# Short-convolution mixer by Strassen products: product 5 of the out-projection in seven parts, with new orders and earlier splits

## The chip, the cores and the metric

The kernel runs on one NeuronCore of a Trainium2 chip. The metric is the time of one execution on the device in microseconds (us), here the median of three runs.

## The reference

What is computed, with T = 1024 tokens and D = 2048 channels, all in float32:

```python
h = rmsnorm(x, norm0_w)
proj = h @ w_in                                   # 2048 x 8192
b_gate, c_gate, u, z = jnp.split(proj, 4, axis=-1)
cu = c_gate * u
conv = causal_depthwise_conv3(cu, w_conv)         # over tokens
y = b_gate * conv * jax.nn.silu(z)
x = x + y @ w_out                                 # 2048 x 2048
return rmsnorm(x, norm_f_w)
```

## The kernel before

All matrix products run on TensorE with float32 operands that are split in two (a rounded high part `h` and the rest `l`); each product is three passes, high x high, low x high, high x low (`PASSES`). `split` makes the parts: ScalarE casts the high part (L113), VectorE subtracts it from the source (L114). A split tile has the form `hl`: two times 1024 columns.

The program is a list of **steps**. A step is 24 matmuls of 128x128 weights on 512 columns, with hooks for its loads, its sums of weights (`add`), its splits, its matmuls and the evacuation of its PSUM banks. The main loop at the end of the kernel calls the loads of a step several steps ahead, its sums four and its splits three steps ahead, then the matmuls and the evacuation of the step itself. After each step it also runs two pieces of `background` work and, in phase 0, one `chore` that prepares later operands. A scheduler then fixes, when the program is built, the order of the instructions on each engine and which buffer each tile gets; each engine runs its own list in that order. Buffers of 4 KB per partition come from the pool `t4` (16), split tiles from `xp` (14, tokens) and `wp` (3, weights), PSUM tiles from 8 banks.

- **In-projection.** The first channel block (c = 0) runs in 8 steps by plain products (L370). Blocks c = 1 to 15 follow twice, in phase 0 for one half of the contraction and in phase 1 for the other, each as seven Strassen products in the order `PRODUCTS` = 1, 5, 6, 2, 7, 3, 4 (L483). The weight of product 5 is the difference `wt` = `wi_01 - wi_00`, made by VectorE (L117); that of product 6 is made from `wt`, that of product 4 in the same tile later. Phase 0 writes the four gate tiles `g` of a block to DRAM (`pd`), phase 1 loads them again and adds its own part from the banks `pa`, `pb`, `pc` (L120).
- **Gating.** When block c of phase 1 is done, `gating(c, g)` goes into `background` and is worked off in the next block: `g_0` times `g_1` (L218), three taps of the convolution (L221 on ScalarE, L225 twice on VectorE), L232, the sigmoid of `g_2` (L231 on ScalarE), L235 that multiplies `g_2` by it, and L238. The sigmoid lies in the tile `g_0`, so L235 is the last to read `g_0`. The result goes to `y_dram`; every second block adds sums of token columns and writes them to `s_dram`, every fourth (c = 3, 7, 11, 15) loads those of the other blocks and makes the sums `z` for the second level (256 columns each, L117 and L120), which go to `zd`.
- **Out-projection.** Products of the first level: 1, 6, 7 and 5, each for two column halves `db` as four steps `out_step` (L601). Products 2, 3 and 4 are taken a second level down, as seven products `out_second` (L670), a step each. So there are 32 + 21 = 53 steps. A step `out_step` loads a weight tile `wo` (512 KB) and a token tile `ys` (512 KB) and splits both; a step `out_second` loads `yz` (512 KB) and two `wz` (512 KB each) and splits all three. Results are added to the output rows `st` (L120), squared for the final norm (L557), and when the last column chunk of a row block has come, `finish` (L753 to L768) makes the scale and stores the rows.
- **Start.** The norm weights `n0` are loaded on ScalarE's queue (L81), tokens `xr` and first weights `wi_c` on SyncE's; ScalarE scales and casts the tokens (L349, needs `n0`), VectorE makes their low part (L350) and splits the weights (L355, L356).

Of the kernel before, what the change touches and what calls it, by code (L numbers as in the profile page):

```python
# [13 lines left out]
P = 128  # L14
# [29 lines left out]
def hybrid_kernel(  # L44
# [36 lines left out]
    nc.scalar.dma_start(n0, norm0_w)  # L81
# [6 lines left out]
    nc.scalar.activation(table, idle[:, 0:1], AF.Sigmoid)  # L88
# [124 lines left out]
    def gating(c, g):  # L213
# [32 lines left out]
        if c == 0:  # L246
            return parts
        if c % 2 == 0:
            kept[c] = gb
            return parts  # L250
# [4 lines left out]
        def s12():  # L255
            add(gc[:, u], e[:, v], gb[:, v])
            sub(gc[:, v], gc[:, u], e[:, u])
            nc.gpsimd.dma_start(sd[:, 0:2], gc.rearrange("p (i n) -> p i n", i=2))

        def s34():  # L260
            sub(gu[:, u], e[:, u], e[:, v])
            sub(gu[:, v], gb[:, u], gc[:, v])
            nc.gpsimd.dma_start(sd[:, 2:4], gu.rearrange("p (i n) -> p i n", i=2))

        if c % 4 == 1:
            return parts + [s12, s34]
        q = {}

        def before():
            q["y"], q["s"] = f4(f"zy_{c}"), f4(f"zs_{c}")  # L270
            nc.sync.dma_start(q["y"], y_dram[c - 2])
            nc.sync.dma_start(q["s"][:, 0:NB], s_dram[c // 4, 0][:, 3])

        def second(z):
            def f():
                t = {2: None, 3: gz, 4: gc}[z]
                if t is None:
                    t = f4(f"z_{c}")
                a = {2: q["y"][:, u], 3: q["s"][:, u], 4: q["y"][:, v]}[z]
                b = {2: gb[:, u], 3: gu[:, v], 4: gb[:, v]}[z]  # L280
# [9 lines left out]
        return [before] + parts + [s12, s34, second(3), second(2), second(4)]  # L290
# [6 lines left out]
    def classical():  # L297
# [241 lines left out]
    ycols = (slice(0, NB), slice(NB, T))  # L539
    yv = y_dram.rearrange("(u j h) p t -> h p u j t", j=2, h=2)  # L540
    sv = s_dram.rearrange("u j p s t -> u p j s t")

    to_come, pending = {}, {}
# [5 lines left out]
    def result(th, tb, chunk, ps):  # L549
# [7 lines left out]
        nc.scalar.activation(idle, v, AF.Square, accum_out=sums[th, tb][:, chunk:chunk + 1])  # L557
        weighs = pending.setdefault((th, tb), [])
        if len(weighs) == 3:
            for f in weighs:  # L560
                f()
            finish(th, tb, chunk)
            return
# [8 lines left out]
        scaled.append(weigh)  # L572

    def out_step(r, db, u):
# [3 lines left out]
        def loads():  # L578
            w["b"] = f4(f"wo_{db}_{r}_{u}")
            nc.sync.dma_start(w["b"], w_out[db, 0, 0, u] if r == 1 else t_dram[r][db, u])  # L580
            w["y"] = f4(f"ys_{db}_{r}_{u}")
            src = yv[0, :, u, :, ycols[0]] if r == 1 else sv[u, :, :, S_SLOT[r]]
            nc.sync.dma_start(w["y"].rearrange("p (j t) -> p j t", j=2), src)

        def split_w():
# [10 lines left out]
        def mm():  # L596
            open_banks()
            for jj in range(2):
                for tb in range(4):
                    for yz, wz in PASSES:  # L600
# [4 lines left out]
                            start=(r in (1, 5) and u == 0 and jj == 0 and yz == 0 and wz == 0),  # L605
                            stop=(r in (7, 5) and u == 3 and jj == 1 and yz == 1),
# [266 lines left out]
```

## Time and profile before

| | |
|---|---|
| median of 3 runs | 1541.2 us (1541.03 to 1541.26) |
| the profiled execution | 1541.5 us |
| its span, first to last instruction | 1539.7 us |
| TensorE busy | 1523.5 us, 99% of the span |
| VectorE busy | 1143.7 us, 74% |
| ScalarE busy | 542.0 us, 35% |
| DMA | 351.95 MB, 229 GB/s over the span |

The profiled execution is 1.8 us longer than its span, and 0.3 us above the median. Busy shares are means over the whole span; a wait of TensorE, in the list of waits, is time in which its next matmul was held up by the named instruction of another engine.

### The profile page before, as it was taken

To read this page: it belongs to the slowest core of one execution; us is meant where nothing else is said; L and a number is where in the kernel's file an instruction comes from. 1 tells how busy PE (TensorE), PEld (TensorE's weight loads), DVE (VectorE), ACT (ScalarE), POOL (GpSimd) and SP (SyncE) were. 2 spreads that over 40 slices of the span, in tenths; PEclk is the share of its full clock that TensorE was granted. 3 is DMA by queue.
4 is the path that set the end of the run, shared out by engine and by line. 5 is a ranking of instruction groups with operands and counts; after the bars stand their busy time and mean duration, and the time that the engine had idled before them with its cause. 6 is when DMAs were issued, how large, how long until landed. Compare 5 with 4: busy or idle time off the path is not lost.

```text
span 1539.7 us, 17753 instructions
## 1 busy us (share of the span) xinstructions
PE 1523.5 (99%) x6705; PEld 1257.5 (82%) x6705; DVE 1143.7 (74%) x1321; ACT 542.0 (35%) x660; POOL 128.2 (8%) x234
## 2 busy tenths in 40 slices
PE   9999999999999999999999999999999999999997
PEld 7878888888888888888888888888888887888885
DVE  6798776677666565457888878887888786687787
ACT  5454444333333333322222222222222334454574
POOL 0001111111111110110000000000000120000000
PEclk9999999999999999999999999999999999999998
DMA  9605677998866674894346434543454679877772
GB/s 362 254 25 205 229 265 266 390 372 331 336 240 251 218 254 157 313 398 150 126 142 203 151 117 139 202 155 112 163 179 164 242 253 385 302 239 233 237 275 109
DMA packets 114277, 351.95 MB, mean 229 GB/s; under 512 B 11008, under 2 KB 22288, under 8 KB 112400
## 3 DMA queue, kind: packets, MB, share of 16 engines
q1 hardware_dynamic: 81040, 223.38, 42.9%
q0 software_dynamic: 31712, 122.72, 20.6%
q10 hardware_dynamic: 1440, 4.73, 0.8%
q8 instruction: 52, 0.85, 0.2%
q14 instruction: 33, 0.27, 0.0%
HBM read 243.83 MB, written 106.96 MB: 228 GB/s over the span
## 4 chain that ended last, share of the span: by engine, by line
PE 90%; DMA 5%; DVE 4%; issue 1%; ACT 1%; SPq 0%; POOL 0%; POOLq 0%; DVEq 0%; ACTq 0%
PE pa L483 42%; PE pc L483 21%; PE pb L483 11%; PE po L601 9%; PE po L670 7%; DMA xsq<-in_x_dram 2%; DMA wz<-in_w_out_dram 1%; DMA xr<-in_x_t_dram 1%; DVE X L114 1%; DVE xr L148 0%; DVE st L120 0%; DVE xc L350 0%; DVE g L397 0%; DMA wi_c<-in_w_in_dram 0%; DVE st L569 0%
## 5 line engine op out<-in xcount | busy, mean ns | idle before, releaser
L483 PE MATMUL pa<-X,w 128*128 128x512 f32 x2880 | 667.8, 389 | 1.1 <-ACT w L113 1.1
L483 PEld LDWEIGHTS pa<-X,w 128*128 128x128 f32 x2880 | 540.5, 188 | 113.8 <-ACT w L113 1.6
L483 PE MATMUL pc<-X,w 128*128 128x512 f32 x1440 | 336.5, 389 | 0.7 <-ACT w L113 0.7
L483 PEld LDWEIGHTS pc<-X,w 128*128 128x128 f32 x1440 | 270.2, 188 | 57.2 <-ACT w L113 1.1
L114 DVE TENSOR_TENSOR w<-wi,w 128x1024 fp32r<-128x1024 f32 x150 | 183.2, 1222 | 146.5 <-ACT w L113 145.5
L113 ACT CAST w<-wi 128x1024 fp32r<-128x1024 f32 x150 | 157.0, 1050 | 229.3 <-PE pa L483 131.4
L601 PE MATMUL po<-wo,Y 128*128 128x512 f32 x768 | 177.5, 389 | 0.9 <-DVE wo L114 0.9
L601 PEld LDWEIGHTS po<-wo,Y 128*128 128x128 f32 x768 | 144.1, 188 | 31.2 <-DVE wo L114 1.4
L483 PE MATMUL pb<-X,w 128*128 128x512 f32 x720 | 168.1, 389 | 0.0
L483 PEld LDWEIGHTS pb<-X,w 128*128 128x128 f32 x720 | 135.1, 188 | 28.1
L113 ACT CAST w<-wt 128x1024 fp32r<-128x1024 f32 x60 | 63.3, 1055 | 234.5 <-PE pc L483 120.2
L120 DVE TENSOR_TENSOR g<-pa,g 128x512 f32<-128x512 f32 x150 | 102.4, 685 | 29.3 <-PE pa L483 28.1
L670 PE MATMUL po<-wzh,Yz 128*128 128x512 f32 x504 | 117.3, 389 | 0.0
L670 PEld LDWEIGHTS po<-wzh,Yz 128*128 128x128 f32 x504 | 94.6, 188 | 19.6
L509 ACT COPY g<-pa 128x512 f32<-128x512 f32 x90 | 52.8, 587 | 138.0 <-PE pa L483 137.7
L117 DVE TENSOR_TENSOR wt<-wi,wi 128x1024 f32<-128x1024 f32 x60 | 73.3, 1222 | 26.7 <-DMA s_dram<-g 14.6
L370 PE MATMUL pc<-xc,wc 128*128 128x512 f32 x384 | 87.9, 390 | 0.9 <-DVE wc L355 0.9
L370 PEld LDWEIGHTS pc<-xc,wc 128*128 128x128 f32 x384 | 71.8, 188 | 17.4 <-issue 1.8
L114 DVE TENSOR_TENSOR w<-wt,w 128x1024 fp32r<-128x1024 f32 x60 | 73.1, 1219 | 10.0 <-ACT w L113 10.0
L120 DVE TENSOR_TENSOR g<-pc,g 128x512 f32<-128x512 f32 x90 | 61.4, 684 | 23.4 <-PE pc L483 23.0
L114 DVE TENSOR_TENSOR wzh<-wz,wzh 128x1024 fp32r<-128x1024 f32 x42 | 50.9, 1219 | 21.2 <-ACT wzh L113 21.1
L120 DVE TENSOR_TENSOR st<-po,st 128x512 f32<-128x512 f32 x90 | 57.5, 682 | 2.6 <-PE po L670 1.9
(106 smaller groups left out, 1030.6 us busy)
## 6 DMA issues: line engine op xcount, KB each, us to landing
wi<-in_w_in_dram SPq DMA_DIRECT2D x120, 512.0 KB, 5.1
pd<-g POOLq DMA_DIRECT2D x60, 512.0 KB, 6.0
g<-pd SPq DMA_DIRECT2D x60, 512.0 KB, 4.5
wp<-in_w_out_dram SPq DMA_DIRECT2D x32, 512.0 KB, 8.1
td<-wp POOLq DMA_DIRECT2D x32, 512.0 KB, 6.8
xd<-xo POOLq DMA_DIRECT2D x28, 512.0 KB, 6.0
X<-xd POOLq DMA_DIRECT2D x14, 1024.0 KB, 10.6
w<-wq POOLq DMA_DIRECT2D x24, 512.0 KB, 4.0
```

The costliest lines, as they stand in the source:

```text
L113: nc.scalar.copy(h, raw)
L114: nc.vector.tensor_tensor(l, raw, h.bitcast(F32), op=ALU.subtract)
L117: nc.vector.tensor_tensor(o, a, b, op=ALU.subtract)
L120: nc.vector.tensor_tensor(o, a, b, op=ALU.add)
L370: nc.tensor.matmul(state["ps"][2 * s + gi][h], wv[:, wz, gi, jj, s, :], xs[:, xz, h * NB:(h + 1) * NB], start=(a == 0 and jj == 0 and wz = ...
L483: nc.tensor.matmul(ps[where, s], wv[:, wz, j, s, :], xt[:, j % 2, xz, :], start=(r in (1, 5, 2) and j == 0 and wz == 0 and xz == 0), stop= ...
L509: nc.scalar.copy(o, ps[where, s])
L601: nc.tensor.matmul(po[first + tb], w["yh"][:, yz, jj * NB + tb * P:jj * NB + (tb + 1) * P], w["w"][:, wz, jj * NB:(jj + 1) * NB], start=(r ...
L670: nc.tensor.matmul(po[2 * pair + tb], w["yh"][:, yz, u * 256 + tb * P:u * 256 + (tb + 1) * P], w["w"][u // 2][:, wz, (u % 2) * NB:(u % 2 + ...
```

## The change

1. **Product 5 of the out-projection in seven parts.** `OUT_PRODUCTS` loses (5, 0) and (5, 1), `SECOND` gets product 5. There are 24 steps `out_step` and 28 steps `out_second`, 52 in all. `SECOND_AFTER` says how many second-level steps follow each first-level step. The seven parts of product 5 need their own token sums (`second(5)` in gating, four of 256 columns in c = 3, 7, 11, 15) and weight sums (`second_weights(5, u)` among the chores), and each of its results goes into two output blocks.
2. **Token operands split once.** For products 1, 6 and 7 the token tiles were loaded and split for each `db`. Now `parted` splits them once, as 512 columns at the end of a block's gating, and writes high and low part to `h_dram` (`hd`, 512 KB each, 24 of them). A step `out_step` loads its split tile `Y` (1 MB, on GpSimd's queue) in place of `ys` and its split.
3. **Background.** Three pieces per step where more than 12 wait.
4. **Start.** `n0` is loaded on SyncE's queue after the first token tile, the first two `wi_c` on ScalarE's queue, the table of ScalarE after them.
5. **End.** The last second-level product takes its parts in the order 1, 5, 6, 3, 2, 7, 4, both last ones row block by row block. Partial sums of squares are added up when three of the four chunks are there (`part`), `finish` needs one operation after the fourth, all results of a step stand ahead of its finishes, and for one row block the far half is scaled on VectorE.

Lines of the new kernel behind L200 are two and more higher: L114, L117 and L120 are L116, L119 and L122 there, L232 and L235 are L234 and L237, L483 is L497.

```diff
-OUT_PRODUCTS = ((1, 0), (5, 0), (6, 0), (7, 0), (5, 1), (1, 1), (6, 1), (7, 1))
-SECOND = ((2, 3, 4), (1, 5, 6, 3, 7, 2, 4))
-NO_SECOND_AFTER = (0, 1, 9, 13, 17)
+OUT_PRODUCTS = ((1, 0), (6, 0), (7, 0), (1, 1), (6, 1), (7, 1))
+SECOND = (2, 5, 3, 4)
+PARTS = (1, 5, 6, 3, 7, 2, 4)
+LAST_PARTS = (1, 5, 6, 3, 2, 7, 4)
+SECOND_AFTER = (0, 0, 0, 1, 0, 0, 0, 1, 2, 1, 2, 1, 2, 1, 2, 1, 2, 1, 2, 1, 1, 2, 2, 3)
...
-    nc.scalar.dma_start(n0, norm0_w)
...
-    nc.scalar.activation(table, idle[:, 0:1], AF.Sigmoid)
...
+    h_dram = {r: dram.tile([4, P, 2, 2, NB], F32R, name=f"hd_{r}") for r in (1, 6, 7)}
+    s_dram = dram.tile([4, 2, P, NB], F32, name="s_dram")
+    s1_dram = dram.tile([4, 2, P, NB], F32, name="s1_dram")
...
+        def parted(r, src):
+            def f():
+                t = t4.tile([P, 2, NB], F32R, name=f"h_{c}_{r}", tag="t4")
+                split(src, t[:, 0, :], t[:, 1, :])
+                nc.gpsimd.dma_start(h_dram[r][c // 4][:, :, (c // 2) % 2], t)
+            return f
+
         if c % 2 == 0:
-            kept[c] = gb
-            return parts
+            if c:
+                kept[c] = gb
+            return parts + [parted(1, gb[:, 0:NB])]
...
+        sums = [parted(6, gc[:, v]), parted(7, gu[:, u])]
         if c % 4 == 1:
-            return parts + [s12, s34]
+            return parts + [s12, s34] + sums
...
-                t = {2: None, 3: gz, 4: gc}[z]
+                t = {2: None, 3: gz, 4: gc, 5: None}[z]
                 if t is None:
-                    t = f4(f"z_{c}")
+                    t = f4(f"z_{c}_{z}")
...
-        return [before] + parts + [s12, s34, second(3), second(2), second(4)]
+        return [before] + parts + [s12, s34] + sums + [second(3), second(2), second(5), second(4)]
...
-                                    nc.sync.dma_start(o, w_in[1, c, 0, gi][:, jj * 256:(jj + 1) * 256])
+                                    (nc.sync if jj else nc.scalar).dma_start(o, w_in[1, c, 0, gi][:, jj * 256:(jj + 1) * 256])
+                                if jj == 0:
+                                    nc.sync.dma_start(n0, norm0_w)
+                                    nc.scalar.activation(table, idle[:, 0:1], AF.Sigmoid)
...
             w["yh"] = hl(xp, f"Y_{db}_{r}_{u}")
-            split(w["y"], w["yh"][:, 0, :], w["yh"][:, 1, :])
+            nc.gpsimd.dma_start(w["yh"].rearrange("p z (j t) -> p z j t", j=2), h_dram[r][u])
...
         def evac():
-            for tb in range(2):
-                result(*dest[tb], po[2 * pair + tb])
+            ends = [result(*d, po[2 * pair + tb]) for tb in range(2) for d in dest[tb]]
+            for f in ends:
+                if f:
+                    f()
...
-        nc.vector.tensor_reduce(tot, sums[th, tb], axis=mybir.AxisListType.X, op=ALU.add)
-        nc.vector.tensor_scalar(tot, tot, 1.0 / D, EPS, op0=ALU.mult, op1=ALU.add)
+        nc.vector.tensor_scalar(tot, sums[th, tb][:, chunk:chunk + 1], 1.0 / D, part[th, tb], op0=ALU.mult, op1=ALU.add)
...
-        nc.scalar.activation(sv[:, far], sv[:, far], AF.Copy, scale=r)
+        if (th, tb) == (1, 2):
+            nc.vector.tensor_scalar(sv[:, far], sv[:, far], r, None, op0=ALU.mult)
+        else:
+            nc.scalar.activation(sv[:, far], sv[:, far], AF.Copy, scale=r)
...
-        for _ in range(3 if i < 12 else 2):
+        for _ in range(3 if i < 12 or len(background) > 12 else 2):
```

Three places show how the change moves instructions. The first is VectorE's list in phase 1 where block 4 passes into block 5, before the change (`wt_5` is the weight difference of product 5 of block 5, `w_5_5` its split tile, `w_5_1` the split tile of product 1, `g_0_5301` to `g_3_5409` the gate tiles of block 4, `z_5694` a token sum of block 3):

```order
L117 TENSOR_TENSOR z_5694<-z_5694,zy_5501 128x256
L117 TENSOR_TENSOR wt_5_5705<-wi_5_01_5579,wi_5_00_5540 128x1024
L117 TENSOR_TENSOR z_5694<-g_3_5170,z_5694 128x256
...
L117 TENSOR_TENSOR wi_5_00_5540<-wi_5_11_5617,wt_5_5705 128x1024
L120 TENSOR_TENSOR g_3_5409<-pc_4_1_5561,g_3_5409 128x512
L114 TENSOR_TENSOR w_5_5_5737<-wt_5_5705,w_5_5_5737 128x1024
L117 TENSOR_TENSOR wt_5_5705<-wi_5_10_5661,wi_5_00_5540 128x1024
L120 TENSOR_TENSOR g_0_5301<-pa_4_0_5510,g_0_5301 128x512
L218 TENSOR_TENSOR g_0_5301<-g_0_5301,g_1_5340 128x1024
```

and the same place after it (`g_0_5359` to `g_3_5471` are the gate tiles of block 4, `g_0_5607` the first of block 5):

```order
L122 TENSOR_TENSOR g_0_5359<-pa_4_0_5574,g_0_5359 128x512
L220 TENSOR_TENSOR g_0_5359<-g_0_5359,g_1_5398 128x1024
L122 TENSOR_TENSOR g_2_5435<-pa_4_1_5587,g_2_5435 128x512
L227 SCALAR_TENSOR_TENSOR g_1_5398<-g_0_5359,wc,g_1_5398 128x1023
L227 SCALAR_TENSOR_TENSOR g_1_5398<-g_0_5359,wc,g_1_5398 128x1022
L122 TENSOR_TENSOR g_0_5607<-pa_5_0_5849,g_0_5607 128x512
L234 TENSOR_TENSOR g_3_5471<-g_3_5471,g_1_5398 128x1024
L237 TENSOR_TENSOR g_2_5435<-g_2_5435,g_0_5359 128x1024
...
L119 TENSOR_TENSOR wt_5_5771<-wi_5_01_5644,wi_5_00_5605 128x1024
L119 TENSOR_TENSOR z_2_5765<-g_3_5228,z_2_5765 128x256
L119 TENSOR_TENSOR wi_5_00_5605<-wi_5_11_5683,wt_5_5771 128x1024
L116 TENSOR_TENSOR w_5_5_5814<-wt_5_5771,w_5_5_5814 128x1024
```

`wt_5` and the low part of `w_5_5` stood ahead of the last additions of block 4 and of its gating; they now stand behind the gating of block 4 up to L237 and behind the addition that reads the first half of product 1 of block 5 (`pa_5_0`). The tile `wt_5` has the buffer that `g_0_5359` had. The lists at blocks 9 and 13 read the same.

The second place is TensorE's list at product 5 of block 5, before the change:

```order
L483 MATMUL pa_5_1_5785<-X_1_0_4360,w_5_1_5707 128x512 x6
L483 MATMUL pa_5_1_5785<-X_1_1_4362,w_5_1_5707 128x512 x6
L483 MATMUL pc_5_0_5811<-X_5_0_4395,w_5_5_5737 128x512 x6
L483 MATMUL pc_5_0_5811<-X_5_1_4397,w_5_5_5737 128x512 x6
L483 MATMUL pc_5_1_5824<-X_5_0_4395,w_5_5_5737 128x512 x6
```

and after it:

```order
L497 MATMUL pa_5_1_5862<-X_1_0_4410,w_5_1_5773 128x512 x6
L497 MATMUL pa_5_1_5862<-X_1_1_4412,w_5_1_5773 128x512 x6
L497 MATMUL pc_5_0_5888<-X_5_0_4445,w_5_5_5814 128x512 x2
L497 MATMUL pc_5_1_5901<-X_5_0_4445,w_5_5_5814 128x512
L497 MATMUL pc_5_0_5888<-X_5_0_4445,w_5_5_5814 128x512 x4
L497 MATMUL pc_5_0_5888<-X_5_1_4447,w_5_5_5814 128x512 x6
```

One matmul that needs only the high part has been drawn ahead of those that need the low part. Blocks 9 and 13 have the same pattern, no other block of phase 1 has it.

The third place is the start of VectorE's list, before the change (`xc` are the scaled tokens, `wc_0` the split weights of the first step):

```order
L350 SCALAR_TENSOR_TENSOR xc_0_209<-xr_179,n_72,xc_0_209 128x512
L355 CAST wc_0_208<-wi_c_0_178 128x2x256
L356 TENSOR_TENSOR wc_0_208<-wi_c_0_178,wc_0_208 128x2x256
L350 SCALAR_TENSOR_TENSOR xc_0_209<-xr_179,n_72,xc_0_209 128x512
```

and after it:

```order
L369 CAST wc_0_214<-wi_c_0_182 128x2x256
L370 TENSOR_TENSOR wc_0_214<-wi_c_0_182,wc_0_214 128x2x256
L364 SCALAR_TENSOR_TENSOR xc_0_215<-xr_183,n_72,xc_0_215 128x512 x2
```

The split of the first weights no longer stands behind the tokens' low part.

## Rows read from the trace of the kernel before

**Rows 1.** Page: the span, and busy time, share and instructions of each engine

```profile
span 1539.7 us, 17753 instructions
PE 1523.5 (99%) x6705; PEld 1257.5 (82%) x6705; DVE 1143.7 (74%) x1321; ACT 542.0 (35%) x660; POOL 128.2 (8%) x234
```

**Rows 2.** Waits of TensorE: us in total, times, longest

```profile
PE pa L483 <- ACT w L113: 1.1, 1, 1.1
PE po L601 <- DVE wo L114: 0.9, 1, 0.9
PE pc L483 <- ACT w L113: 0.7, 1, 0.7
```

**Rows 3.** Chain that ended last, one piece of 1480 to 1517: start, us, what

```profile
1490.30 5.44 PE po L670 x24
```

**Rows 4.** Timeline of the start: start us, us, engine, [idle before, releaser]

```profile
1.19 0.89 SPq L316 DMA_DIRECT2D wi_c<-in_w_in_dram  x2
...
3.74 0.72 ACT L349 ACTIVATE xc<-xr,n 128x512 fp32r<-128x512 f32 x1 [1.06 <-DMA n<-in_norm_w_dram]
...
5.52 0.43 DVE L355 CAST wc<-wi_c 128x512 fp32r<-128x512 f32 x1 [0.28 <-DMA wi_c<-in_w_in_dram]
...
6.10 1.13 PE L370 MATMUL pc<-xc,wc 128*128 128x512 f32 x3 [0.89 <-DVE wc L355]
```

**Rows 5.** Timeline of the end, 1522 to 1535

```profile
1521.64 6.74 PE L670 MATMUL po<-wzh,Yz 128*128 128x512 f32 x29
...
1531.26 0.61 ACT L557 ACTIVATE idle<-st 128x512 bf16<-128x512 f32 x1
...
1533.00 1.15 ACT L765 ACTIVATE st<-st,r 128x1024 f32<-128x1024 f32 x1 [1.03 <-POOL r L756]
...
1534.18 0.37 ACTq L768 DMA_DIRECT2D out_dram<-st  x1
```

**Rows 6.** Timeline of VectorE, 1286 to 1296, ahead of TensorE's wait in the out-projection

```profile
1288.34 4.87 DVE L120 TENSOR_TENSOR st<-po,st 128x512 f32<-128x512 f32 x8
```

**Rows 7.** Timelines of VectorE, ScalarE and TensorE where block 4 passes into block 5

```profile
808.73 0.41 DVE L117 TENSOR_TENSOR z<-z,zy 128x256 f32<-128x256 f32 x1
812.84 1.23 DVE L117 TENSOR_TENSOR wt<-wi,wi 128x1024 f32<-128x1024 f32 x1 [3.70 <-DMA zd<-g]
...
819.52 1.21 DVE L114 TENSOR_TENSOR w<-wt,w 128x1024 fp32r<-128x1024 f32 x1
...
814.58 1.06 ACT L113 CAST w<-wt 128x1024 fp32r<-128x1024 f32 x1 [4.43 <-PE pc L483]
...
814.34 11.04 PE L483 MATMUL pa<-X,w 128*128 128x512 f32 x48
825.22 5.60 PE L483 MATMUL pc<-X,w 128*128 128x512 f32 x24
```

**Rows 8.** Timelines of TensorE and VectorE where block 15 passes into the out-projection

```profile
1238.66 17.61 PE L601 MATMUL po<-wo,Y 128*128 128x512 f32 x77
...
1238.86 0.69 DVE L120 TENSOR_TENSOR g<-pa,g 128x512 f32<-128x512 f32 x1 [0.77 <-PE pa L483]
1239.47 1.27 DVE L225 SCALAR_TENSOR_TENSOR g<-g,wc,g 128x1023 f32<-128x1023 f32 x1
...
1243.10 1.23 DVE L232 TENSOR_TENSOR g<-g,g 128x1024 f32<-128x1024 f32 x1
1244.25 1.23 DVE L235 TENSOR_TENSOR g<-g,g 128x1024 f32<-128x1024 f32 x1
```

**Rows 9.** Windows of the out-projection: busy times, granted clock, DMA share, GB/s

```profile
1238.70:1254.00 15.30, 15.30 (x69) 12.69 (x68) 14.26 (x21) 5.65 (x6) 2.70 (x5) 1.00 0.36 140
1254.00:1326.00 72.00, 71.05 (x314) 58.52 (x313) 52.24 (x57) 32.17 (x32) 7.31 (x11) 1.00 1.04 376
```

**Rows 10.** Windows at the end: us, TensorE busy, granted clock, DMA share, GB/s

```profile
1531.60:1531.80 0.20, 0.00 (x0) 0.76 1.15 451
1531.80:1532.00 0.20, 0.00 (x0) 0.50 1.02 369
```

More of the change, by code (lines that the diff above doesn't have):

```diff
@@ L537, in open_banks @@
             po.extend(bank(f"po_{i}") for i in range(8))
-    ycols = (slice(0, NB), slice(NB, T))
     yv = y_dram.rearrange("(u j h) p t -> h p u j t", j=2, h=2)
-    sv = s_dram.rearrange("u j p s t -> u p j s t")
-    to_come, pending = {}, {}
+    to_come, pending, complete, part = {}, {}, {}, {}
     def expect(blocks):
@@ L557, in result @@
         nc.scalar.activation(idle, v, AF.Square, accum_out=sums[th, tb][:, chunk:chunk + 1])
+        got = complete.setdefault((th, tb), [])
+        got.append(chunk)
+        if len(got) == 3:
+            t = part[th, tb] = const.tile([P, 1], F32, name=f"part_{th}_{tb}")
+            s = sums[th, tb]
+            nc.vector.tensor_tensor(t, s[:, got[0]:got[0] + 1], s[:, got[1]:got[1] + 1], op=ALU.add)
+            nc.vector.tensor_tensor(t, t, s[:, chunk:chunk + 1], op=ALU.add)
+            nc.vector.tensor_scalar(t, t, 1.0 / D, EPS, op0=ALU.mult, op1=ALU.add)
         weighs = pending.setdefault((th, tb), [])
@@ L561, in result @@
                 f()
-            finish(th, tb, chunk)
-            return
+            return lambda: finish(th, tb, chunk)
         todo = [chunk]
@@ L572, in result @@
         scaled.append(weigh)
+        return None
     def out_step(r, db, u):
@@ L604, in mm @@
                             w["w"][:, wz, jj * NB:(jj + 1) * NB],
-                            start=(r in (1, 5) and u == 0 and jj == 0 and yz == 0 and wz == 0),
-                            stop=(r in (7, 5) and u == 3 and jj == 1 and yz == 1),
+                            start=(r == 1 and u == 0 and jj == 0 and yz == 0 and wz == 0),
+                            stop=(r == 7 and u == 3 and jj == 1 and yz == 1),
                             skip_group_check=True,
@@ L614, in evac @@
                 for th, dh in dest:
-                    result(th, tb, 2 * dh + db, po[first + tb])
+                    f = result(th, tb, 2 * dh + db, po[first + tb])
+                    if f:
+                        f()
         return Step(loads, nothing, split_w, mm, evac)
@@ L621, in out_second @@
         w = {}
-        half, dh = {2: (1, 0), 3: (1, 1), 4: (1, 0)}[z]
-        th = {2: 0, 3: 0, 4: 1}[z]
+        half, dh = {2: (1, 0), 3: (1, 1)}.get(z, (None, None))
+        blocks = {2: [(0, 0)], 3: [(0, 1)], 4: [(1, 0)], 5: [(0, 1), (1, 1)]}[z]
         def loads():
@@ L661, in out_second @@
         t2, db2 = {1: (0, 0), 5: (1, 1), 6: (0, 1), 2: (0, 0), 7: (1, 1), 3: (0, 1), 4: (1, 0)}[p]
-        dest = [(th, 2 * t2 + tb, 2 * dh + db2) for tb in range(2)]
-        expect(dest)
-        end = z == 4 and p == 4
+        dest = [[(th, 2 * t2 + tb, 2 * d + db2) for th, d in blocks] for tb in range(2)]
+        expect(dest[0] + dest[1])
+        end = z == SECOND[-1] and p in (7, 4)
         def mm():
@@ L687, in second_weights @@
         q = []
-        half, dh = {2: (1, 0), 3: (1, 1), 4: (1, 0)}[z]
+        half, dh = {2: (1, 0), 3: (1, 1)}.get(z, (None, None))
         def load():
@@ L692, in load @@
                 q.append(f4(f"wq_{z}_{u}_{db}"))
-                nc.sync.dma_start(q[db], t_dram[4][db, u] if z == 4 else w_out[db, half, dh, u])
+                nc.sync.dma_start(q[db], t_dram[z][db, u] if z in t_dram else w_out[db, half, dh, u])
         def sums13():
@@ L777, in hybrid_kernel @@
     one = [out_step(r, db, u) for r, db in OUT_PRODUCTS for u in range(4)]
-    two = [out_second(z, p) for z in SECOND[0] for p in SECOND[1]]
+    two = [out_second(z, p) for z in SECOND for p in (LAST_PARTS if z == SECOND[-1] else PARTS)]
     for i, step in enumerate(one):
         steps.append(step)
-        if i >= 8 and i - 8 not in NO_SECOND_AFTER:
+        for _ in range(SECOND_AFTER[i]):
             steps.append(two.pop(0))
-    steps.extend(two)
     in_second = [i for i in range(8 + 7, 8 + 7 * 14)]
@@ L794, in hybrid_kernel @@
             chores.extend(out_weights(db, u))
-    for z in (2, 3, 4):
+    for z in SECOND:
         for u in range(4):
-            chores.extend(second_weights(z, u))
+            parts = second_weights(z, u)
+            if (z, u) != (SECOND[0], 0):
+                parts[0:1] = [lambda a=chores.pop(), b=parts[0]: (a(), b())]
+            chores.extend(parts)
     chore_at = {in_second[i]: f for i, f in enumerate(chores)}
```

35 lines of the change are left out of this document (16 added, 19 removed).

## The prediction, made before the changed kernel was run

> **What bounds the kernel now.** First the page: TensorE is busy 1523.5 us of a span of 1539.7 us, 99% [rows 1]. Then the end of the chain of waits: steps of 24 matmuls follow each other, 5.44 us each [rows 3], so a matmul costs 0.227 us and the time is the number of matmuls, plus what lies ahead of the first, plus what lies behind the last, plus gaps. Third, the waits of TensorE: 1.1, 0.9 and 0.7 us behind the start [rows 2], under 3 us in 1.5 ms. Ahead lie 6.10 us, of which 0.89 us is a wait for the first weights [rows 4]. The last matmul ends at 1521.64 + 6.74 = 1528.38, and 11.3 us of finishing follow [rows 5]. So a saving has to come out of the matmul count, the ends or those gaps, while every new wait of TensorE counts in full, since nothing gives it back.
>
> VectorE and ScalarE are off the path with 74% and 35% [rows 1], but they make each step's weights. What matters there is not the amount of work but its order: an engine takes its list in order, so an operation that waits holds up the splits behind it.
>
> **The change part by part.** The sum is made against the profiled execution, 1541.5 us; the median is 0.3 us lower.
>
> *Matmuls.* Before, product 5 took 8 steps, now 7: 53 steps become 52, 24 matmuls less. One step at 5.44 us [rows 3]: **-5.4**.
>
> *Start.* The first matmul waits for the weights' cast, which waits at 5.52 for `wi_c`, issued at 1.19 behind another transfer [rows 4]. On ScalarE's queue it can go about 0.4 us earlier, and the weights' split no longer stands behind the tokens' low part. Against this, `n0` goes out later, and ScalarE's first operation waited for it until 3.74 [rows 4], 2.4 us ahead of the matmul. I take **-0.4**; bounds -0.9 (the whole wait) and +0.9 (`n0` comes later than the cover).
>
> *End.* In the last row block the square that feeds the scale is done only from 1531.26 on, 2.9 us behind the last matmul, since ScalarE scales another row first; the last scaling starts at 1533.00 and the last store is issued at 1534.18 [rows 5]. The new `finish` has one operation fewer on the chain, squares ahead of scalings, and for one row a scaling on VectorE. Behind the last matmul the shortest chain of the same operations is about 0.9 us shorter. Bounds: 0, and -2.9 if that late square starts at once. Taken: **-0.9**. Banks of the last two products are used again without a step between; the addition that frees them has some 13 matmuls (2.9 us) for operations of 0.7 us, so no wait is taken there.
>
> *Wait in the out-projection.* The 0.9 us behind `wo` [rows 2] come from eight additions in a row, 4.87 us of VectorE, ahead of the split [rows 6]: the end of product 5 of the first level, which is gone. **-0.9**; bounds -0.9 and 0.
>
> *More work on VectorE, ScalarE and queues.* The 24 early splits, the token sums of product 5, its weight sums and 12 more additions to `st` are hidden as long as they stand behind no wait: VectorE has 396 us idle. Where that cover fails is the next point and the rival on the out-projection. In block 1 of phase 0 a token split stands behind a weight cast now; the largest wait of that region is 1.1 us [rows 2]. Bounds 0 and 1.1, taken **+0.2**.
>
> *A new wait in phase 1.* This term decides. Before, VectorE made `wt_5` at 812.84, held up 3.70 us by a DMA write of `zd` that still read the buffer; the low part of its split was done at 820.7, and product 5 began at 825.22, right behind product 1, without waiting [rows 7]. Block 5 began 10.88 us (two steps) after 814.34, less one step: at 819.78. So `wt_5` was made 7 us ahead of its block. In the new list it stands behind L237 of block 4 and behind an addition that reads the first half of product 1 of block 5. That gating can only begin when block 4 is complete. A passage without other work between shows its speed, block 15 into the out-projection, with t = 0 at 1238.66 [rows 8]:
> - the last addition of the block at +0.20, the first tap L225 at +0.81; two taps of 1.27 us, 1.2 us apart, end at +3.3;
> - the addition from `pa_5_0` (its matmuls end at +2.72) takes 0.69 us, then L234 starts at about +3.8 and L237 1.15 us later (the distance of the two rows at 1243.10 and 1244.25), at +4.95, so that it ends at +6.1;
> - three additions for `z`, 0.41 us long and about 0.33 apart [rows 7], then `wt_5` from +7.1 to +8.3 (1.23 us [rows 7]);
> - ScalarE's cast, 1.06 us [rows 7], ends at about +9.5.
>
> Product 5 could start at +5.44. TensorE waits **4.1 us**. It can then do three matmuls with the high part (0.7 us; the list of TensorE has just this third one drawn forward), until +10.2. The low part comes behind `z`, the sum in `wi_00` and its own subtraction: from +8.3 another 0.3 + 1.15 + 1.15, so at about +10.9. Another **0.75 us**. Together 4.85 us in block 5, and by the same lists in blocks 9 and 13: **+14.6**. Bounds: if the taps did not hold it up, the chain from `pa_5_0` alone gives 2.9 + 0.6 + 1.15 + 1.15 + 1.0 + 1.2 + 1.1 = 9.1, that is 3.7 us and no second wait, 11.1 in all; with one more split of 1.2 us let in between, 6.05 us each, 18.2 in all. Nothing gives it back, as TensorE has no reserve in these blocks.
>
> *The clock after such a wait.* The clock is at its full level, 2.4 GHz, wherever TensorE works. At the end it had fallen to 0.50 of it, 1.2 GHz, in the window from 1531.80, 3.4 us behind the last matmul [rows 10]. A wait of 4.1 us is a little longer than that, so it can fall here too, and the next matmuls would take twice the time. No row shows matmuls at the low level. Bounds for each wait: 0, and 5.44 us (a whole product at half speed). As the wait is just over the only example, I take a quarter of one product for all three: **+1.4**.
>
> The Trainium skill, "TensorE: Matmul & The Clock Gate", section "HAM oscillation — how this bites in real kernels", says that a matmul engine which waits for its data between bursts is set back to the low clock, and that each burst then starts there; the rule speaks against this change. The row of the end agrees that idleness lowers the clock. By that rule each of the three waits would be paid for twice, once idle and once slow; this is one of the rivals.
>
> *Out-projection.* Each first-level step now loads 1.5 MB in place of 1 MB. Before, from 1254 to 1326 the DMA engines were full (1.04, 376 GB/s), and from 1238.7 to 1254 they moved only 140 GB/s [rows 9]. New steady need: 1.57 MB in 5.44 us, 289 GB/s, under the 376. The first 16 steps (87 us) need some 6.8 MB more (11 first-level steps with 0.52 MB more each, and two second-level steps of 1.57 MB in the place of first-level ones of 1.05). Bounds: 0 if it is spread over the idle stretch, 6.8 MB / 376 GB/s = 18.1 us if nothing hides. Nearer to 0, since the idle stretch alone holds (376 - 140) x 15.3 us = 3.6 MB and the load runs ahead. Taken **+1.5**.
>
> Sum: 1541.5 - 5.4 - 0.4 - 0.9 - 0.9 + 0.2 + 14.6 + 1.4 + 1.5 = 1551.6, less 0.3 to the median: **1551.3 us**.
>
> **The rivals.**
> - *A. It does what it is meant to (not slower).* `wt` is ready in time in blocks 5, 9 and 13, because its place in the list behind L237 does not cost: for this the gating of the block before would have to be done by +3.1 (so that 1.23 and 1.06 us fit in ahead of +5.44), while rows put L237's end at +6.1. Time: 1541.2 - 5.4 - 0.4 - 0.9 - 0.9 + 0.2 + 1.5 = 1535.3, and 1533.8 without the out-projection's term. It decides from a wait under about 2.5 us per block on, which is where the 7.4 us of savings less the +0.2 are used up. For it: VectorE is only 74% busy. Against it: the order is fixed, and each link has its row. Chance 0.07.
> - *B. A tie.* The wait is at its lower bound (11.1), the clock stays up, the out-projection costs nothing and the end gives its full 2.9 us: 1541.2 - 9.6 + 0.2 + 11.1 = 1542.9. Chance 0.08.
> - *C. The out-projection becomes bound by DMA.* Of the 6.8 MB only 3.6 MB find room; 3.2 MB / 376 GB/s = 8.5 us in place of 1.5: 1558.3. For it: 1.04 for 72 us [rows 9]. Against: in that stretch the loads were also catching up. Chance 0.15.
> - *D. The clock falls in all three waits.* Half a product to a whole one at the low level each: 1551.3 - 1.4 + 8.2 to 16.3 = 1558 to 1566. For it: [rows 10]; against: the wait is only a little longer than what that row shows. Chance 0.12.
>
> **How the numbers follow.** Forecast 0.58, A 0.07, B 0.08, C 0.15, D 0.12. About 0.2% (3.1 us) is what a measurement of this kernel can tell from no change. Faster by more: A, 0.07. Within it, 1538.1 to 1544.3: B, 0.08. Slower: the rest, 0.85. The forecast's own bounds are 1545 (11.1 for the wait, 0 for clock and out-projection) to 1555 (18.2 for the wait). The range takes in part of B below and most of D above: 1544 to 1561.
>
> **What would show it.** In the changed kernel's waits of TensorE: product 5 (`pc`, L497) behind ScalarE's cast of `w` three times with about 4.1 us, and behind VectorE's low part three times with about 0.75 us, at about 825, 982 and 1139 us (blocks are 152.3 us apart, and each wait shifts the next). VectorE's `wt` there right behind L237. TensorE has 6672 matmuls besides the 9 at the start. The end behind the last matmul is 10.4 us. Windows behind the three waits show the granted clock at 1.00; at 0.5, D is right. New waits of `po` behind DMA of `Y` or `wz` from 1250 to 1340 would be C. The forecast is wrong if `wt` comes early, if the waits are much shorter, or if a wait that I have not seen stands elsewhere.

## The result, and the profile after

The changed kernel takes 1563.6 us (median of four runs, 1562.8 to 1564.8) against 1541.2 before: 1.0144 times, interval 1.0132 to 1.0156. It is slower by 22.4 us, where 10.1 were forecast, and lies above the range of 1544 to 1561. Its profiled execution took 1563.3 us with a span of 1561.4. The page, beside [rows 1]:

```profile
span 1561.4 us, 17973 instructions
PE 1528.8 (98%) x6681; PEld 1259.1 (81%) x6681; DVE 1162.0 (74%) x1387; ACT 537.7 (34%) x664; POOL 167.8 (11%) x294
```

There are 24 matmuls less, yet TensorE is busy 5.3 us longer: some matmuls ran slowly. The waits of TensorE (total, times, longest), beside [rows 2]:

```profile
PE pc L497 <- ACT w L115: 12.0, 3, 4.0
PE po L618 <- ACT Yz L115: 3.6, 1, 3.6
PE po L618 <- DMA Y<-hd: 3.0, 2, 2.5
...
PE pc L384 <- DVE xc L364: 0.8, 1, 0.8
PE pa L497 <- ACT w L115: 0.7, 1, 0.7
```

The first row is the wait that was forecast: three times, 4.00 us each. The second and third stand in the out-projection. TensorE's timeline shows both places, and what follows the waits:

```profile
817.69 6.28 PE L497 MATMUL pa<-X,w 128*128 128x512 f32 x27
827.97 8.44 PE L497 MATMUL pc<-X,w 128*128 128x512 f32 x24 [4.00 <-ACT w L115]
836.25 5.60 PE L497 MATMUL pa<-X,w 128*128 128x512 f32 x24
...
987.29 7.35 PE L497 MATMUL pc<-X,w 128*128 128x512 f32 x24 [4.00 <-ACT w L115]
...
1145.52 8.39 PE L497 MATMUL pc<-X,w 128*128 128x512 f32 x24 [4.00 <-ACT w L115]
...
1286.96 12.77 PE L618 MATMUL po<-wo,Y 128*128 128x512 f32 x48 [2.49 <-DMA Y<-hd]
1300.27 11.16 PE L618 MATMUL po<-wo,Y 128*128 128x512 f32 x48 [0.54 <-DMA Y<-hd]
...
1320.42 7.31 PE L618 MATMUL po<-wo,Y 128*128 128x512 f32 x24 [3.55 <-ACT Yz L115]
```

A step of 24 has a row of 5.60 us (matmul rows overlap their successors by 0.16). The steps behind the waits have 8.44, 7.35 and 8.39 us. Windows of TensorE around the first (us, busy, granted clock, DMA share, GB/s) show why:

```profile
824.00:825.00 1.00, 0.00 (x0) 1.00 0.00 0
...
826.00:827.00 1.00, 0.00 (x0) 0.84 0.00 0
827.00:828.00 1.00, 0.03 (x1) 0.50 0.00 0
...
833.00:834.00 1.00, 1.00 (x5) 0.74 0.78 131
834.00:835.00 1.00, 1.00 (x6) 1.00 0.87 352
```

TensorE stopped at 823.97. Before it resumed, the clock fell to 1.2 GHz, and it stayed there for 5.5 us of work. The same stands behind the second and the third wait:

```profile
988.00:989.00 1.00, 1.00 (x4) 0.50 1.03 422
...
1146.00:1147.00 1.00, 1.00 (x4) 0.50 0.94 385
```

**Where the time went**, on the two spans (+21.7 us). In blocks 5, 9 and 13 the stretch from the end of product 1 to the next product is 12.28, 11.19 and 12.22 us in place of 5.28: +19.8, of which 12.0 are waits. In the out-projection: waits of 6.6 us, and steps at the low clock that took 12.77 us for 10.88 and 7.15 for 5.44, +3.6; the old wait of 0.9 us is gone. Matmuls -5.4. Start and block 1 together -1.4: block 5 starts at 818.4 in place of 819.8. End -0.7 (10.6 us behind the last matmul in place of 11.3 [rows 5]). Together 19.8 + 6.6 + 3.6 - 0.9 - 5.4 - 1.4 - 0.7 = 21.6; the last 0.1 is rounding.

### The profile page after: what moved, and what is told of

Read it like the earlier page. It is cut to its first block, busy times and chain, and to the rows that moved or that the text cites. A ratio compares the mean times of both kernels' runs of the same rounds, so it can differ in the third digit from the quotient of the medians.

```text
span 1561.4 us, 17973 instructions
## 1 busy us (share of the span) xinstructions
PE 1528.8 (98%) x6681; PEld 1259.1 (81%) x6681; DVE 1162.0 (74%) x1387; ACT 537.7 (34%) x664; POOL 167.8 (11%) x294
## 4 chain that ended last, share of the span: by engine, by line
PE 93%; DMA 2%; DVE 2%; issue 1%; ACT 0%; POOL 0%; SPq 0%; POOLq 0%; DVEq 0%; ACTq 0%
PE pa L497 41%; PE pc L497 21%; PE pb L497 10%; PE po L689 9%; PE po L618 6%; PE pc L384 6%; DMA wz<-w 2%; DMA Y<-hd 1%; DVE g L227 0%; DVE g L234 0%; DVE g L122 0%; DVE g L237 0%; ACT w L115 0%; DMA xr<-in_x_t_dram 0%; DVE wt L119 0%
## 5 line engine op out<-in xcount | busy, mean ns | idle before, releaser
L497 PE MATMUL pa<-X,w 128*128 128x512 f32 x2880 | 667.8, 389 | 0.7 <-ACT w L115 0.7
L497 PEld LDWEIGHTS pa<-X,w 128*128 128x128 f32 x2880 | 540.5, 188 | 113.4 <-ACT w L115 1.1
L497 PE MATMUL pc<-X,w 128*128 128x512 f32 x1440 | 343.9, 395 | 12.0 <-ACT w L115 12.0
L497 PEld LDWEIGHTS pc<-X,w 128*128 128x128 f32 x1440 | 274.1, 191 | 72.3 <-ACT w L115 13.3
L116 DVE TENSOR_TENSOR w<-wi,w 128x1024 fp32r<-128x1024 f32 x150 | 183.6, 1224 | 138.1 <-ACT w L115 137.4
L497 PE MATMUL pb<-X,w 128*128 128x512 f32 x720 | 168.1, 389 | 0.0
L497 PEld LDWEIGHTS pb<-X,w 128*128 128x128 f32 x720 | 135.1, 188 | 28.1
L689 PE MATMUL po<-wzh,Yz 128*128 128x512 f32 x672 | 155.2, 389 | 0.0
L689 PEld LDWEIGHTS po<-wzh,Yz 128*128 128x128 f32 x672 | 126.1, 188 | 26.2
L618 PE MATMUL po<-wo,Y 128*128 128x512 f32 x576 | 137.2, 396 | 6.6 <-ACT Yz L115 3.6
L122 DVE TENSOR_TENSOR g<-pa,g 128x512 f32<-128x512 f32 x150 | 103.1, 688 | 45.3 <-PE pa L497 45.0
L618 PEld LDWEIGHTS po<-wo,Y 128*128 128x128 f32 x576 | 110.1, 192 | 31.0 <-ACT Yz L115 3.9
L116 DVE TENSOR_TENSOR wzh<-wz,wzh 128x1024 fp32r<-128x1024 f32 x56 | 67.9, 1222 | 23.4 <-ACT wzh L115 23.2
L122 DVE TENSOR_TENSOR g<-pc,g 128x512 f32<-128x512 f32 x90 | 61.9, 689 | 28.6 <-PE pc L497 28.5
L119 DVE TENSOR_TENSOR wt<-wi,wi 128x1024 f32<-128x1024 f32 x60 | 73.3, 1222 | 13.0 <-DMA hd<-h 10.9
L116 DVE TENSOR_TENSOR w<-wt,w 128x1024 fp32r<-128x1024 f32 x60 | 73.3, 1222 | 10.9 <-ACT w L115 10.9
L115 ACT CAST wzh<-wz 128x1024 fp32r<-128x1024 f32 x56 | 58.4, 1050 | 51.0 <-PE po L689 26.8
```

The lines of the kernel that those rows point to most:

```text
L115: nc.scalar.copy(h, raw)
L116: nc.vector.tensor_tensor(l, raw, h.bitcast(F32), op=ALU.subtract)
L119: nc.vector.tensor_tensor(o, a, b, op=ALU.subtract)
L122: nc.vector.tensor_tensor(o, a, b, op=ALU.add)
L497: nc.tensor.matmul(ps[where, s], wv[:, wz, j, s, :], xt[:, j % 2, xz, :], start=(r in (1, 5, 2) and j == 0 and wz == 0 and xz == 0), stop= ...
L618: nc.tensor.matmul(po[first + tb], w["yh"][:, yz, jj * NB + tb * P:jj * NB + (tb + 1) * P], w["w"][:, wz, jj * NB:(jj + 1) * NB], start=(r ...
```

## Experiments

Two questions stood open: whether the place of `wt` makes the three waits, and what delays the out-projection. Each time is a median beside the kernel before on the same chip. The ratio's interval stands behind it.

| kernel | us | before | interval of the ratio |
|---|---|---|---|
| e_wt | 1550.3 | 1541.2 | 1.0039 to 1.0072 |
| e_nopart | 1553.1 | 1541.2 | 1.0067 to 1.0101 |
| **e_nopart_wt** | **1533.9** | 1541.2 | 0.9937 to 0.9967 |
| e_warm | 1560.0 | 1541.2 | 1.0106 to 1.0136 |
| e_z5 | 1563.5 | 1541.0 | 1.0132 to 1.0163 |
| e_z5_gu | 1544.3 | 1540.6 | 1.0010 to 1.0028 |
| e_wt_yhalf | 1547.9 | 1541.0 | 1.0034 to 1.0065 |
| e_wt_early | 1547.2 | 1541.0 | 1.0025 to 1.0057 |
| e_wt_stlate | 1550.3 | 1540.6 | 1.0046 to 1.0076 |
| e_wt_early_stlate | 1550.0 | 1540.6 | 1.0047 to 1.0080 |
| e_wt_early7 | 1545.1 | 1541.6 | 1.0013 to 1.0033 |
| e_wt_early7_yhalf | 1540.1 | 1541.6 | 0.9978 to 0.9997 |

### The three waits in phase 1

**e_wt**: one buffer less.

```diff
-                t = {2: None, 3: gz, 4: gc, 5: None}[z]
+                t = {2: None, 3: gz, 4: gc, 5: gu}[z]
```

> The changed kernel with one edit: the token sums of product 5 (second(5)) go into the gate tile g_1, which is done with by then, so no extra buffer is taken, and wt of blocks 5, 9, 13 gets the buffer of another tile and no longer stands behind L237 of the block before. Theory (the buffer order makes the three waits): the waits of product 5 behind the cast of wt are gone, and the slow clock behind them too; in the changed kernel's trace the three products 5 take 12.28, 11.35 and 12.38 us from the end of product 1 on in place of 5.44 each, 19.7 us too much, so about 1563.6 - 19.7 = 1544 us. Rival (VectorE has too much to do with the early splits and is late whatever the buffers): the waits stay or come up elsewhere in these blocks, 1558 to 1564 us.

Measured 1550.3 us. The waits of TensorE:

```profile
PE po L618 <- DMA Y<-hd: 6.2, 2, 5.5
PE pc L497 <- DVE w L116: 2.2, 3, 0.7
...
PE pc L497 <- ACT w L115: 1.1, 2, 0.9
```

The three waits of 4.0 us are gone: the buffer makes them. Small ones stay at the same places: 0.74 us three times for the low part and 1.1 us for the cast, since `wt` comes later than before the change, and behind those of block 13 (0.85 us and 0.74 us) 22 matmuls took 1.6 us too long, at a clock that had fallen (the last section shows it). By TensorE's timeline the three stretches are still 1.4, 1.5 and 3.8 us too long, 6.7 in place of 19.8, while the out-projection lost some 1.5 us less than in the changed kernel. These two account for 5.2 of the 6.3 us over the expectation; the rest lies within the scatter of the runs, 1546.5 to 1552.1.

**e_nopart**: token operands loaded unsplit and split for each `db` as before the change, product 5 in seven parts.

```diff
-            return parts + [parted(1, gb[:, 0:NB])]
+            return parts
...
-        sums = [parted(6, gc[:, v]), parted(7, gu[:, u])]
+        sums = []
...
-            nc.gpsimd.dma_start(w["yh"].rearrange("p z (j t) -> p z j t", j=2), h_dram[r][u])
+            split(w["y"], w["yh"][:, 0, :], w["yh"][:, 1, :])
```

> The changed kernel without its second part: token operands of products 1, 6 and 7 are loaded unsplit and split for each column half as before; product 5 stays in seven parts. wt of blocks 5, 9, 13 keeps its place behind L237. Theory (the three waits come from the extra tile of product 5's sums, those in the out-projection from the 1 MB loads of split tokens): the three waits of 4 us in phase 1 stay, the waits on Y in the out-projection go; there the changed kernel lost 6.6 us of waits and some 3.5 us of slow clock, so 1563.6 - 10.1 = 1553.5 us. Rival (the early splits make VectorE late in phase 1): the three waits go with them, and the time is about 1534 us. Second rival (the out-projection is held up by its new order, not by the loads): about 1563 us.

**e_nopart_wt**: both edits.

> Both edits: the token sums of product 5 in the gate tile g_1, and no early splits. Theory: both losses go, 1563.6 - 19.7 - 10.1 = 1533.8 us, the 5.4 us of the 24 matmuls and some 2 us at start, end and block 1 below the kernel before. Rival (another wait takes their place, as the splits of the out-projection are again on VectorE): 1537 to 1545 us.

Measured 1553.1 and 1533.9 us, each within 0.5 us of the theory; as the runs scatter from 1552.1 to 1556.4 and from 1532.4 to 1535.2, that closeness is in part luck. The waits of e_nopart, then of e_nopart_wt:

```profile
PE pc L488 <- ACT w L113: 12.0, 3, 4.0
...
PE pc L488 <- DVE w L114: 0.4, 1, 0.4
...
PE po L684 <- DVE wzh L114: 0.2, 1, 0.2
```

```profile
PE pa L488 <- ACT w L113: 0.7, 1, 0.7
PE po L613 <- ACT Yz L113: 0.2, 1, 0.2
```

The early splits have no part in the waits of phase 1, and theirs are the waits of the out-projection. Without the early splits and without the extra tile, what is left of the change is faster than the kernel before by 7.3 us; the forecast had added up 7.4 us of savings without the new waits. This is the fastest version.

**e_z5** and **e_z5_gu**: the kernel before, with the token sums of product 5 made and stored, not used (with the load of what they are made from); in a tile of their own, and in the control in `gu`, the gate tile g_1.

```diff
-                t = {2: None, 3: gz, 4: gc}[z]
+                t = {2: None, 3: gz, 4: gc, 5: None}[z]
...
-        return [before] + parts + [s12, s34, second(3), second(2), second(4)]
+        return [before] + parts + [s12, s34, second(3), second(2), second(5), second(4)]
```

> The kernel before with one addition: in the gating of blocks 3, 7, 11 and 15 the token sums of product 5 are made too (four of 256 columns, into a tile of their own, stored like the other sums and not used; the out-projection is that of before). Theory (one more tile in the pool of 16 buffers is what pushes wt of blocks 5, 9, 13 back): three waits of about 4 us behind the cast of wt, each followed by the low clock, as in the changed kernel, where they cost 19.7 us: 1541.2 + 19.7 = 1560.9 us, a little less if the low part comes earlier. Rival (the waits need the new order of the out-projection, of the chores or of the background): no waits, 1541 to 1543 us.

> The control to e_z5: the kernel before with the same token sums of product 5, the same four operations and the same store, but in the gate tile g_1, so that no tile is added to the pool. Theory (the extra tile alone makes the three waits of 5.67 us that e_z5 shows): no waits in blocks 5, 9, 13 and the time of the kernel before, 1541 to 1542 us. Rival (the work and the store themselves make VectorE late): the waits stay, 1555 to 1563 us.

Measured 1563.5 and 1544.3 us. The waits of e_z5, one of its three places on TensorE's timeline, then the waits of the control:

```profile
PE pc L484 <- ACT w L113: 17.9, 4, 5.7
```

```profile
832.52 7.77 PE L484 MATMUL pc<-X,w 128*128 128x512 f32 x24 [5.67 <-ACT w L113]
```

```profile
PE po L602 <- DVE wo L114: 2.7, 1, 2.7
PE pa L484 <- DVE g L120: 1.2, 1, 1.2
```

One tile more in the pool of 16, with four short operations, costs the kernel before 22.6 us; the same operations without the tile cost 3.7 (one other wait is longer by 1.8 us, one of 1.2 us is new) and no wait in blocks 5, 9 and 13. In e_z5 `wt` stands still further back, behind the new sums, so the waits are 5.67 us and the forecast 2.6 us short.

**e_warm**: TensorE kept at work in the wait.

```diff
+                    if r == 5 and s == 0 and ph == 1 and c in (5, 9, 13):
+                        for _ in range(12):
+                            nc.tensor.matmul(ps[where, s], idle[:, 0:P], idle, start=True, stop=True)
```

> The changed kernel with 12 more bf16 matmuls of 512 columns ahead of product 5 in blocks 5, 9 and 13, into the bank that product 5 starts afterwards, so that TensorE is idle 4.0 - 12 x 0.22 = 1.4 us there. Theory (most of what these waits cost beyond their 4.0 us is the clock, which falls when TensorE stands still that long): the clock stays at its full level, product 5 takes 5.44 us again plus the 0.75 us for the low part; per block 6.84, 5.91 and 6.94 us become 4.75, together 5.4 us less: 1558.2 us. Rival (the products are long because their weights come late, not because of the clock): no change, 1563.6 us, and the windows behind the waits still show what they showed.

Timeline of TensorE at the first place, then windows there:

```profile
828.22 1.21 PE L500 MATMUL pc<-X,w 128*128 128x512 f32 x4 [1.39 <-ACT w L115]
829.70 0.50 PE L500 MATMUL pa<-X,w 128*128 128x512 f32 x1 [0.27 <-ACT w L115]
830.03 4.72 PE L500 MATMUL pc<-X,w 128*128 128x512 f32 x20
834.60 5.38 PE L500 MATMUL pa<-X,w 128*128 128x512 f32 x23
```

```profile
826.00:827.00 1.00, 0.82 (x4) 1.00 0.00 0
...
828.00:829.00 1.00, 0.78 (x3) 1.00 0.24 98
```

The clock stays at 1.00 in all three places, and the matmuls of product 5 have their normal pace. From the end of product 1 (824.22 here) the three stretches are 4.9 us too long each (14.6 in place of 19.8; one matmul of the next product, the row of 829.70, is drawn into them and taken off). So 5.2 of the 19.8 us are the clock's, for 5.4 expected, and 14.6 are paid at the full clock too. The median is lower by 3.6 us, the profiled execution by 4.3: the out-projection waits 1.0 us longer here (7.6 us).

### The out-projection

In the changed kernel the DMA engines have room while the last gating runs and are full from 1280 on (windows: busy times of the engines, clock, DMA share, GB/s), beside [rows 9], and GpSimd's queue holds the tiles `Y` behind the stores of the last gating (its timeline):

```profile
1260.00:1270.00 10.00, 10.00 (x45) 8.27 (x45) 9.93 (x14) 3.71 (x5) 1.68 (x3) 1.00 0.45 145
...
1280.00:1328.00 48.00, 41.41 (x166) 33.00 (x165) 22.82 (x25) 12.41 (x14) 7.50 (x12) 0.93 1.05 394
```

```profile
1265.95 0.58 POOL L241 DMA_DIRECT2D y_dram<-g  x1 [18.77 <-DVE g L240]
...
1276.48 0.55 POOL L606 DMA_DIRECT2D Y<-hd  x1
```

The tile issued at 1276.48 is the one that TensorE needed at 1284.5 and got at 1287.0. So there are two suspects: too many bytes, and issue too late. All that follows stands on e_wt.

**e_wt_yhalf**: half the bytes of each `Y`.

```diff
-            nc.gpsimd.dma_start(w["yh"].rearrange("p z (j t) -> p z j t", j=2), h_dram[r][u])
+            nc.gpsimd.dma_start(w["yh"][:, 0].rearrange("p (j t) -> p j t", j=2), h_dram[r][u][:, 0])
...
-                            w["yh"][:, yz, jj * NB + tb * P:jj * NB + (tb + 1) * P],
+                            w["yh"][:, 0, jj * NB + tb * P:jj * NB + (tb + 1) * P],
```

> The kernel e_wt (buffer of wt set right) with the high part alone of each split token tile loaded in the first-level steps of the out-projection, 512 KB in place of 1 MB, at the same place of the same queue; its matmuls take the high part where the low part belonged, so the low part's share of these products is left out, and the count of matmuls is the same. In e_wt the out-projection lost 6.2 us waiting for these tiles and 2.4 us to the low clock behind it. Theory (too many bytes for the DMA engines from 1260 to 1328): the waits go, 1550.3 - 8.6 = 1541.7 us. Rival (the loads are issued too late, since GpSimd's queue has the stores of the last gating in front of them): most of the waits stay, 1546 to 1550 us.

**e_wt_early**: `Y` for the first six first-level steps issued ahead of the last gating (`pre` allocates the tile and issues its load).

```diff
...
+        if i == first_out - 1:
+            for k in (0, 1, 2, 3, 5, 6):
+                steps[first_out + k].pre()
         s.evac()
```

> The kernel e_wt with the loads of split tokens for the first six first-level steps of the out-projection issued before the last block's gating, so that on GpSimd's queue they stand ahead of its stores; same bytes. Theory (bytes): the load of the DMA engines only moves by some 2 MB into the stretch before, which had some room (0.82 of them busy from 1238 to 1262), so part of the wait goes or moves to later tiles: 1544 to 1549 us. Rival (late issue alone): the waits go, 1541.7 us.

Measured 1547.9 and 1547.2 us: neither is the cause alone. The longest wait of each:

```profile
PE po L618 <- DMA Y<-hd: 6.3, 1, 6.3
```

```profile
PE po L622 <- DMA Y<-hd: 4.8, 1, 4.8
```

**e_wt_stlate** and **e_wt_early_stlate**: a third suspect, the row loads `st`, issued six steps later, alone and with the early tiles.

```diff
-            if m in (-1, 0, 4, 5):
+            if m in (-1, 0, 10, 11):
...
-                    open_rows(int(m > 0), tb + 2 * (m in (0, 5)), db)
+                    open_rows(int(m > 0), tb + 2 * (m in (0, 11)), db)
```

> The kernel e_wt with the loads of the second half of the output rows (st, eight transfers of 512 KB for each column half on GpSimd's queue) six steps later, where they are still ahead of their first use. In e_wt and in its variant with half the bytes per token tile, the tile that TensorE waited for was issued right behind two such loads, between others, and landed 13 us later at a full DMA load, while its bytes alone mattered little. Theory (a burst: row loads and the loads that SyncE's queue releases after the last gating share the DMA engines with the one tile that is needed next): the waits on Y in the first part of the out-projection go or fall to under 2 us, 1541.7 to 1544 us. Rival (total bytes over the whole out-projection): 1548 to 1550 us.

> Both edits on e_wt: the first six split token tiles issued ahead of the last gating, and the row loads six steps later. Theory (burst): no wait on Y is left, 1541.7 us or less; what stays above 1533.8 us is the waits of 0.7 us for the low part in blocks 5, 9 and 13 and other small ones. Rival (total bytes): waits come up at later tiles, 1545 to 1548 us.

Measured 1550.3 and 1550.0 us: the suspicion falls. The wait on `Y` shrank or went, and one for weights came in its place, in e_wt_stlate and e_wt_early_stlate:

```profile
PE po L689 <- ACT wzh L115: 5.0, 1, 5.0
```

```profile
PE po L622 <- ACT wo L115: 4.8, 1, 4.8
```

**e_wt_early7** and **e_wt_early7_yhalf**: seven tiles early, with all bytes and with half.

> The kernel e_wt with the split token tiles of seven first-level steps (four of product 1, three of product 6) loaded ahead of the last gating; all bytes as in e_wt. Moving other loads has so far only moved the wait to the next tile or to the weights. Theory (two causes together: the loads are issued late, and afterwards the DMA engines are full, as each step loads 1.5 MB): a wait of 3 to 6 us stays, for a later tile or for weights, 1545 to 1550 us. Rival (late issue alone): no wait above 1 us, about 1541 us.

> The same, with the high part alone of each split token tile loaded, 512 KB in place of 1 MB; the matmuls take the high part where the low part belonged, so the low part's share of these products is left out, the count of matmuls is the same. Theory (late issue and full DMA engines together, since halving the bytes alone left a wait of 6.3 us and issuing early alone one of 4.8 us): the waits in the out-projection go or stay under 1 us, 1540 to 1542 us. Rival (something else holds up these loads, such as the stores of the last gating or the weights on SyncE's queue): a wait of 3 to 6 us stays, 1545 to 1548 us.

Measured 1545.1 and 1540.1 us. The waits of the out-projection in e_wt_early7, then the costliest of TensorE's behind the start in e_wt_early7_yhalf, which stands in phase 1 (the out-projection has none in the list):

```profile
PE po L695 <- DVE wzh L116: 2.9, 1, 2.9
...
PE po L622 <- ACT Yz L115: 2.0, 1, 2.0
```

```profile
PE pc L497 <- DVE w L116: 2.1, 3, 0.7
```

Early issue and half the bytes together leave no wait there; either alone leaves one of 3 to 6 us. So there are two causes, each of which is enough for a wait, and both have to go: while the last gating runs, the engines have room that late issue leaves unused, and afterwards each step has 1.5 MB to load. That the engines are full says little by itself: from 1280 to 1328 their share is 1.06 in e_wt_early7_yhalf too, where TensorE does not wait. Whether still more tiles issued early, with all their bytes, would do was not tried. e_nopart_wt has the bytes of the half tiles, loads them on SyncE's queue up to six steps ahead, and waits 0.2 us.

## Why the prediction was wrong

| step | forecast | measured |
|---|---|---|
| matmuls | -5.4 | -5.4 |
| start | -0.4 | -0.2 |
| block 1 of phase 0 | +0.2 | -1.2 |
| end | -0.9 | -0.7 |
| old wait in the out-projection | -0.9 | -0.9 |
| new wait in phase 1, at full clock | +14.6 | +14.6 (e_warm) |
| clock behind it | +1.4 | +5.2 (19.8 less 14.6) |
| out-projection | +1.5 | +10.2 |

*Right: the sign, and the mechanism that decides.* The chain on VectorE and ScalarE in block 5 can be read off row by row, with t = 0 at 818.4:

```profile
822.29 1.22 DVE L234 TENSOR_TENSOR g<-g,g 128x1024 f32<-128x1024 f32 x1
823.42 1.22 DVE L237 TENSOR_TENSOR g<-g,g 128x1024 f32<-128x1024 f32 x1
...
825.56 1.22 DVE L119 TENSOR_TENSOR wt<-wi,wi 128x1024 f32<-128x1024 f32 x1
...
826.87 1.04 ACT L115 CAST w<-wt 128x1024 fp32r<-128x1024 f32 x1 [3.95 <-DVE wt L119]
```

L234 starts at +3.9, L237 at +5.0, `wt` at +7.2, the matmuls at +9.6; forecast were +3.8, +4.95, +7.1 and +9.5. The wait is 4.00 us for 4.1. The second one, 0.75 us for the low part, is not among the waits of the matmuls: at half speed the first three last nearly until it is ready, and only the weight load behind them waited for it (0.55 us in each of the three places). In e_nopart, where the clock fell later in block 5, the matmuls did wait 0.4 us for the low part. At full clock, in e_warm, the whole delay of a block is 4.9 us for 4.85. So the term was right, 14.6; in the trace of the changed kernel 12.0 of it are idle time.

*Wrong: the clock.* The step that failed is "I take a quarter of one product for all three". The row of the end showed a fall 3.4 us behind the last matmul [rows 10], and the waits were longer; I still weighed it as the exception. It fell in all three. The stretches are 3.0, 1.9 and 2.9 us too long beyond the 4.00 of idle time, 7.8 in all; e_warm still pays 2.6 of these at full clock, so the clock costs 5.2, for 1.4 forecast. The rule of the Trainium skill, "TensorE: Matmul & The Clock Gate", section "HAM oscillation — how this bites in real kernels", that waits between bursts set the engine back to the low clock and the bursts start there, is what these windows show: 0.50 in all three. Rival D had this case, with 8.2 to 16.3 us; that was too much.

*Wrong: the out-projection.* "Nearer to 0, since the idle stretch alone holds 3.6 MB and the load runs ahead" failed: the load does not run ahead. The tiles `Y` are issued on GpSimd's queue three steps ahead, behind the stores of the last gating, which waited until 1265.95 for VectorE, so the stretch with room passed unused. I had the bytes, and not the queue that they stand in. 8.5 us were forecast in rival C, measured were 10.2, of which 3.6 are the clock again. C and D were given 0.15 and 0.12 as if one excluded the other; they came together. The time, 1563.6, lies beyond C's 1558.3, and inside D's 1558 to 1566 only because C's cost came on top of a smaller one for the clock. The range ended at 1561, so it took in less than half of D, not most of it as the prediction says.

*Small ones.* The first matmul starts 0.7 us earlier, but the next waits 0.83 us for the tokens' low part, since `n0` lands later: the bound of the other side nearly came. The end is 0.7 us shorter for 0.9. In block 1 of phase 0 waits of 1.8 us became 0.7, where a loss of 0.2 was forecast. The 7.4 us of savings in rival A are already less the 0.2.

## What to carry to other kernels

Count live tiles before adding one: in a full pool with a fixed order, one tile can move an unrelated operation behind a long chain, and its own work of four short instructions says nothing of the price. Price a wait of the matmul engine with the clock behind it as a term of its own (here 5.2 us for three waits of 4.00), and when loads move to another queue, look at what stands ahead of them there when the stage begins. Rivals that can both happen need a case of their own.

## What the runs showed of the hardware

The clock's fall and return were uneven for equal waits. Behind three waits of 4.00 us it was back at full level 5.5, 3.2 and 5.4 us after the work resumed. In the out-projection it fell even behind a wait of 2.49 us, and only after the matmuls had begun again (1286.96):

```profile
1286.00:1287.00 1.00, 0.04 (x1) 1.00 1.03 406
1287.00:1288.00 1.00, 1.00 (x4) 0.74 1.04 386
1288.00:1289.00 1.00, 1.00 (x4) 0.50 1.17 428
```

In e_wt it fell in block 13 behind two waits of 0.85 and 0.74 us with two matmuls between them, while 0.22 and 0.74 us in block 9 left it at 1.00:

```profile
1133.86 6.93 PE L497 MATMUL pc<-X,w 128*128 128x512 f32 x22 [0.74 <-DVE w L116]
```

```profile
1135.00:1136.00 1.00, 1.00 (x4) 0.50 0.90 369
```

In e_wt_early7 waits of 2.92 and 1.99 us left it at 1.00. So in these runs the length of the wait alone does not tell whether the clock falls. What decides it was not tried.
